# Program order for all engines, with deferred operations, in two attention stages of a two-layer trunk

## Chip, cores and metric

The kernel runs on one core of one Trainium2 chip. The metric is the time of one execution on the device in microseconds (us). "Before" is the median of three runs.

## What is computed

Two layers of a diffusion trunk over 256 context tokens and 256 latent tokens of 1024 channels. In each layer three token mixers read the same normalised input, and gates merge them:

```python
o_a = mla_attend(...)                    # 8 heads
s = einsum(q, k) * dh ** -0.5            # differential attention: 4 heads, two softmaxes each
a = p[:, :, 0] - lam * p[:, :, 1]
o_b = rms_norm(a @ v, diff_norm) * (1 - lam_init)
o_c = swa(...)                           # 8 heads, window 128, context keys and a sink logit
y = (ga * (o_a @ wa) + gb * (o_b @ wb) + gc * (o_c @ wc)) @ wo
x = x + gate * rms_norm(y)
x = x + gate2 * rms_norm(swiglu(...))
```

Latent queries read all 512 keys, context queries the 256 context keys. In the last layer only the latent tokens are queries. The modulation vectors come from a large product of the conditions with `w_ada`.

## The kernel before, in words

All matrices are float32. A weight block (128 x 1024) is loaded into one of three buffers `raw`, cast on ScalarE (ACT) into a high half, and subtracted on VectorE (DVE) for a low half; both go into one of three buffers `hl` (L131, L132). Each product is then three TensorE (PE) products, high by high, high by low, low by high (`mm3`, L262 to L264).

The work is a list of units, each with its weight blocks. `drive` runs units one after another. A unit is a generator that yields its TensorE cost in microseconds (3 x columns / 2400 for each triple); between the yields `drive` lets two other generators advance: a side, here an attention, which gets `ratio` microseconds of its own cost for each microsecond of the unit's, and a filler, which does the modulation products on VectorE (`ada_dve`: L397, L399, with weights `aw`) at a rate of its own (0.42 in layer 0 here).

An attention is a list of steps, one for each head and tile of 128 queries, and two for the two softmaxes or the two heads of a pair. `attend` interleaves their stages: S scores on TensorE into one of two banks `psS`; E the maximum (L669), the exponential (L673) and, at each second step, the normalisation; T transposes into a bank `psT` and a copy back to `pp` (L689 on ScalarE, L691 on VectorE); V the value products (L696, L776) into `psV`; F the last transposes of a head (differential attention). The score cost of a step is keys x 2 / 2400 us, the ratios in the covered stages are R2 = 0.383 and 0.482 (differential, layers 0 and 1) and R3 = 0.541 and 0.896 (sliding). In the differential attention the transposes and values of a tile come three and four steps behind the scores.

Softmax tiles, gates, rotated projections and small temporaries share six rotating buffers `work`. Rotary tiles take two steps on VectorE (L640, L641), two on GpSimd (POOL; L642, L643), and then casts on ScalarE (L972, L134) and subtractions on VectorE (L973, L135) that split them into `dQA`, `sk`, `sQ`. The differential output is normalised with a copy (L837), squares and a power on GpSimd (L839, L288), sums and a multiply on VectorE (L841, L843).

TensorE and SyncE (SP, which issues the loads) run in the order in which the program emits them. For ScalarE, VectorE and GpSimd a planner sorts the instructions at build time by its own estimate of when each is ready, with E and T at a high priority:

```python
ctx.enter_context(tc.manual_schedule(engines={mybir.EngineType.PE, mybir.EngineType.SP}))
...
with tc.high_priority():
    steps[j - 1]["E"]()
```

Of the kernel before, what the change touches and what calls it, by code (L numbers as in the profile page):

```python
# [19 lines left out]
P = 128  # L20
# [67 lines left out]
def trunk(ctx: ExitStack, tc: tile.TileContext, x, cx, b_ada, attn_post,  # L88
# [39 lines left out]
    def split_into(hi, lo, src, scale=None):  # L128

        if scale is None:  # L130
            nc.scalar.copy(hi, src)  # L131
            nc.vector.tensor_tensor(lo, src, hi.bitcast(F32), ALU.subtract)  # L132
        else:
            nc.scalar.activation(hi, src, AF.Copy, scale=scale)  # L134
            nc.vector.scalar_tensor_tensor(lo, src, scale, hi.bitcast(F32), ALU.mult, ALU.subtract)  # L135

    NHL, NRAW = 3, 3
    units, flat, state = [], [], {"load": 0, "split": 0, "next": 0}
# [33 lines left out]
    def do_split(b):  # L172
# [7 lines left out]
        split_into(b["parts"][0], b["parts"][1], raw, b["scale"])  # L180

    def ahead(idx, live, more):

        live += sum(not b["keep"] for b in flat[idx:state["split"]])
        more -= max(0, state["split"] - idx)
        while state["split"] < len(flat):
            b = flat[state["split"]]
            need = state["split"] < idx
            if not need and (more <= 0 or (live >= NHL and not b["keep"])):
                break  # L190
            while state["load"] <= state["split"]:
                do_load(flat[state["load"]])
                state["load"] += 1
            do_split(b)
# [4 lines left out]
        while state["load"] < min(len(flat), state["split"] + NRAW):  # L199
            do_load(flat[state["load"]])  # L200
            state["load"] += 1
# [33 lines left out]

    def drive(n, side=None, ratio=1.0, at=()):

        acc, t, at = 0.0, 0.0, list(at)
        for _ in range(n):
            for cost in run_unit():  # L240
                fillers(cost)
                acc += cost * ratio
                t += cost
                while at and at[0][0] <= t:
                    at.pop(0)[1]()
                while side is not None and acc > 0:
                    v = next(side, None)
                    if v is None:
                        side = None
                    else:  # L250
                        acc -= v
        for _, f in at:
            f()
        if side is not None:
            for _ in side:
                pass
# [319 lines left out]
    def start():  # L576
        def load():
            do_load(flat[state["load"]])
            state["load"] += 1
# [99 lines left out]
    def p_T(st, nk, act, dst=None):  # L679
# [8 lines left out]
        if act:  # L688
            nc.scalar.copy(dst, src)  # L689
        else:  # L690
            nc.vector.tensor_copy(dst, src)  # L691

    def weigh(st, nk, av, v):
        n = nk // P
# [3 lines left out]
    def out_T(o, f, oT, qts, scale=None):  # L698
# [7 lines left out]
        split_into(*[oT[f // 2][:, f % 2, j, 512 - n:512] for j in range(2)], pt[:, :n], scale)  # L706

    L = [{} for _ in range(DEPTH)]
    WARM = 18
    PRM = {"WN": (44, 16), "DU": (5, 7, 8, 15, 13, 16, 21, 22), "ST": (0.46, 1.61), "FR": (0.42, 0.642, 0.21, 0.134),  # L710
# [6 lines left out]
    def head64_steps(l, env, bn, passes, qk, v, sinks, mask):  # L717
# [3 lines left out]
        for f in range(4):  # L721
            hs = {}
            for t in qts:
                nk = 256 if t < 2 else 512
                pair = {}
                for m in range(2):
# [12 lines left out]
                    def E(st=st, h=h, nk=nk, m=m, pair=pair):  # L739
# [7 lines left out]
                        if sinks:  # L747
# [3 lines left out]
                            nc.vector.tensor_tensor(sm, sm, es, ALU.add)  # L751
                        rs = small([P, 2], "rsd")
                        nc.vector.reciprocal(rs, sm)
                        for j in range(2):
                            p = pair[j]["p"][:, :nk]
                            if j:
                                nc.scalar.activation(p, p, AF.Copy, scale=rs[:, j:j + 1])
                            else:
                                nc.vector.tensor_scalar(p, p, rs[:, j:j + 1], None, ALU.mult)  # L759

                    def T(st=st, nk=nk, m=m, t=t, hs=hs):
# [5 lines left out]
                    if m:  # L767
                        def V(f=f, t=t, nk=nk, hs=hs, pair=pair):
                            if t % 2 == 0:
# [8 lines left out]
                            if t == qts[-1]:  # L778
# [3 lines left out]
                                split_into(*[env["oT", bn][f // 2][:, f % 2, j, cs] for j in range(2)], hs["av"][:, cs])  # L782
# [10 lines left out]
    def diff_steps(l, env):  # L793
        qts, nq = env["qts"], len(env["qts"])
        steps = []
        for h in range(4):
            hs = {}
            for i, t in enumerate(qts):
                nk = 256 if t < 2 else 512
                pair = {}  # L800
                for m in range(2):
# [9 lines left out]
                    def E(st=st, nk=nk, m=m, pair=pair):  # L811
# [5 lines left out]
                        rs = small([P, 2], "rsd")  # L817
                        nc.vector.reciprocal(rs, pair["sm"])
                        nc.vector.tensor_tensor(rs[:, 1:2], rs[:, 1:2], env["lam"], ALU.mult)
                        p0, p1 = pair[0]["p"], pair[1]["p"]  # L820
                        nc.vector.tensor_scalar(p1[:, :nk], p1[:, :nk], rs[:, 1:2], None, ALU.mult)
                        nc.vector.scalar_tensor_tensor(p1[:, :nk], p0[:, :nk], rs[:, 0:1], p1[:, :nk], ALU.mult, ALU.subtract)

                    st.update(S=S, E=E)
                    if m == 1:
                        def T(st=st, nk=nk):
                            p_T(st, nk, 1)

                        def V(st=st, h=h, nk=nk, i=i, hs=hs):
# [10 lines left out]
                            ssd = small([P, 4], "ssd")  # L840
                            nc.vector.tensor_reduce(ssd[:, :nq], sq[:, :nq], AX.X, ALU.add)  # L841
                            rq = rsqrt(ssd[:, :nq], nq, P * EPS)
                            nc.vector.tensor_tensor(ob, ob, rq.rearrange("p (t o) -> p t o", o=1).to_broadcast([P, nq, P]), ALU.mult)  # L843
# [8 lines left out]
    def mixers(l):  # L852
# [115 lines left out]
        def stack_k(A, B, r):  # L968

            for m in range(2):  # L970
                rows, other = slice(64 * m, 64 * m + 64), slice(64 - 64 * m, 128 - 64 * m)
                nc.scalar.copy(A[rows, m], r[rows])  # L972
                nc.vector.tensor_tensor(B[rows, m], r[rows], A[rows, m].bitcast(F32), ALU.subtract)  # L973
                (nc.vector, nc.gpsimd)[m].tensor_copy(A[other, m], A[rows, m].bitcast(F32))
# [6 lines left out]
        def stack_q(Q, r, n0):  # L981

            cs = slice(n0, 512)
            for m in range(2):
                rows, other = slice(64 * m, 64 * m + 64), slice(64 - 64 * m, 128 - 64 * m)
                split_into(Q[rows, m, cs], Q[other, m, cs], r[rows, cs], 0.125)
# [15 lines left out]
        def after(h, f, r):  # L1002
# [3 lines left out]
            else:  # L1006
                f(r)
# [86 lines left out]
        def sk(parts):  # L1094
# [4 lines left out]
            stack_k(env["sA"], env["sB"], env["r"])  # L1099
# [14 lines left out]
        def sq(i):  # L1114
            def f(parts):
# [3 lines left out]
                stack_q(env["sQ", i // 2][:, i % 2], env["r"], TQ0)  # L1119
# [53 lines left out]
        def branch_pair(bi, i):  # L1173
            def f(parts):
# [15 lines left out]
                if bi == 2:  # L1190
                    nc.vector.tensor_tensor(g, a, g, ALU.add)
                    split_into(env["mh", i // 4][at], env["ml", i // 4][at], g, 0.5)
            return f

        def branch(bi, i0):
            def f(parts):
# [5 lines left out]
                for j in range(2):  # L1202
# [9 lines left out]
                    if bi == 2:  # L1212
                        nc.vector.tensor_tensor(g, a, g, ALU.add)
                        split_into(env["mh", i // 4][:, i % 4, TQ0:512], env["ml", i // 4][:, i % 4, TQ0:512], g, 0.5)
# [212 lines left out]
    for l in range(DEPTH):  # L1427
# [22 lines left out]
        else:  # L1450
# [3 lines left out]
        drive(count(("gate", "branch", "s")) - 24, attend(diff_steps(l, env), PRM["LD"][1]), PRM["R2"][l])  # L1454
        swa = head64_steps(l, env, "c", 2, lambda h, t, nk: stacked(env["sQ", h % 4 // 2][:, h % 2], env["sA"], env["sB"], h // 4, t, nk),
                           lambda h, k: env["sv"][:, k * P + 64 * (h // 4):k * P + 64 * (h // 4) + 64],
                           True, lambda t: {2: (3, 0), 3: (2, 1)}.get(t))
        drive(PRM["SWA"][l])
        drive(12 - PRM["SWA"][l], attend(swa, PRM["LD"][2]), PRM["R3"][l])
        drive(8)  # L1460
        flush()
# [64 lines left out]
```

## Time and profile before

| | |
|---|---|
| median of three runs | 1481.27 us (1480.56 to 1482.76) |
| profiled execution, its own time | 1483.21 us |
| its span, first to last instruction | 1481.4 us |
| TensorE busy | 1439.1 us (97%) |
| VectorE busy | 971.9 us (66%) |
| ScalarE busy | 684.3 us (46%) |
| GpSimd busy | 175.8 us (12%) |
| granted TensorE clock, mean | 0.995 |

The differential attention of layer 0 starts at about 198 us, its sliding attention at about 344 us, and the stretch that the change covers ends near 495 us. In layer 1 the stretch is about 1068 to 1246 us. Matmul ends are modelled, so an idle time of TensorE is read from the starts of its instructions.

### The profile page before, as it was taken

The numbers are of one execution on the slowest core, as the hardware profiler recorded it, in microseconds if no ns is written. First come the engines' busy times: TensorE is split into PE (matmuls) and PEld (weight loads), VectorE is DVE, ScalarE is ACT, GpSimd is POOL, SyncE is SP. The second block draws the span as 40 slices with busy tenths as digits, with TensorE's granted clock in tenths as the row PEclk, the third lists the DMA queues.
The fourth block names the chain that finished last, engine by engine and source line by source line (L and its number), as shares of the span: only waits on it lengthen the run. The fifth ranks groups of instructions, "written<-read, shape, count | busy, mean of one in ns | idle before, by whom it ended". The sixth has DMA issues, their size and how long they took to land. (4 is left out here: it accounts for less than half of the span.)

```text
span 1481.4 us, 21891 instructions
## 1 busy us (share of the span) xinstructions
PE 1439.1 (97%) x8434; PEld 1215.3 (82%) x8434; DVE 971.9 (66%) x1646; ACT 684.3 (46%) x1265; POOL 175.8 (12%) x245
## 2 busy tenths in 40 slices
PE   8989999999999999999999999999999899999998
PEld 7867878777777889887778888877798899899986
DVE  4676777878785655879773224779577776666654
ACT  5576554444552355223222223665455655544443
POOL 1262001120000010000000000364003100100000
PEclk9999999999999999999999999999999999999999
DMA  9321322233223542666572334333242536566664
GB/s 350 123 79 44 113 86 100 102 112 128 86 85 129 185 142 96 215 216 209 204 229 97 100 100 148 123 111 128 100 136 86 164 100 217 168 227 208 219 208 162
DMA packets 62728, 216.16 MB, mean 146 GB/s; under 512 B 7048, under 2 KB 7584, under 8 KB 62624
## 3 DMA queue, kind: packets, MB, share of 16 engines
q1 hardware_dynamic: 61184, 210.05, 42.3%
q10 hardware_dynamic: 1440, 4.72, 0.8%
q8 instruction: 66, 1.08, 0.3%
q14 instruction: 38, 0.31, 0.1%
HBM read 209.48 MB, written 5.27 MB: 145 GB/s over the span
## 5 line engine op out<-in xcount | busy, mean ns | idle before, releaser
L262 PE MATMUL psg<-hT,hl 128*128 128x512 f32 (+1 forms) x1328 | 470.6, 354 | 0.0
L264 PE MATMUL psg<-hT,hl 128*128 128x512 f32 (+1 forms) x1328 | 449.1, 338 | 1.0 <-DVE hl L132 1.0
L263 PE MATMUL psg<-hT,hl 128*128 128x512 f32 (+1 forms) x1328 | 448.8, 338 | 0.3 <-DVE hT L460 0.3
L132 DVE TENSOR_TENSOR hl<-raw,hl 128x1024 fp32r<-128x1024 f32 (+2 forms) x251 | 311.7, 1242 | 207.7 <-ACT hl L131 206.8
L131 ACT CAST hl<-raw 128x1024 fp32r<-128x1024 f32 (+2 forms) x251 | 259.1, 1033 | 328.7 <-PE psg L264 167.8
L262 PEld LDWEIGHTS psg<-hT,hl 128*128 128x128 f32 x1328 | 252.4, 190 | 38.7 <-issue 15.4
L264 PEld LDWEIGHTS psg<-hT,hl 128*128 128x128 f32 x1328 | 252.3, 190 | 29.4 <-DVE hl L132 1.4
L263 PEld LDWEIGHTS psg<-hT,hl 128*128 128x128 f32 x1328 | 252.9, 190 | 25.6 <-issue 3.6
L399 DVE SCALAR_TENSOR_TENSOR acc<-aw,siluc,acc 128x512 f32<-128x512 f32 x224 | 163.9, 757 | 22.8 <-DMA aw<-in_ada_rest 21.8
L477 POOL TENSOR_SCALAR smy<-ssy 128x1 f32<-128x1 f32 x12 | 4.1, 340 | 709.0 <-ACT work L293 709.0
L673 ACT ACTIVATE work<-psS,nm 128x512 f32<-128x512 f32 (+1 forms) x96 | 59.2, 617 | 59.4 <-DVE nm L669 31.3
L669 DVE TENSOR_REDUCE nm<-psS 128x1 f32<-128x512 f32 (+1 forms) x96 | 57.0, 596 | 22.1 <-PE psS L735 15.6
L684 PE MATMUL psT<-ca,work 128*128 128x128 f32 x400 | 63.5, 273 | 6.7 <-DVE work L759 4.1
L262 PE MATMUL psg<-oT,hl 128*128 128x512 f32 (+1 forms) x192 | 68.5, 357 | 0.0
L264 PE MATMUL psg<-oT,hl 128*128 128x512 f32 (+1 forms) x192 | 65.3, 340 | 1.6 <-DVE hl L132 1.6
L263 PE MATMUL psg<-oT,hl 128*128 128x512 f32 (+1 forms) x192 | 65.1, 339 | 0.0
L684 PEld LDWEIGHTS psT<-ca,work 128*128 128x128 f32 x400 | 48.5, 141 | 17.2 <-issue 7.3
L262 PE MATMUL psg<-hl,hT 128*128 128x256 f32 (+1 forms) x168 | 57.1, 340 | 1.4 <-ACT hT L131 1.4
L673 ACT ACTIVATE work<-psS,nmd 128x512 f32<-128x512 f32 (+1 forms) x48 | 29.6, 618 | 44.8 <-DVE nmd L669 23.6
L264 PE MATMUL psg<-hl,hT 128*128 128x256 f32 (+1 forms) x168 | 48.0, 286 | 0.4 <-DVE hT L132 0.4
L263 PE MATMUL psg<-hl,hT 128*128 128x256 f32 (+1 forms) x168 | 47.7, 284 | 0.0
L689 ACT COPY pp<-psT 128x512 f32<-128x512 f32 (+1 forms) x72 | 36.7, 510 | 19.3 <-PE psT L684 18.8
(319 smaller groups left out, 2514.1 us busy)
## 6 DMA issues: line engine op xcount, KB each, us to landing
raw<-in_blocks SPq DMA_DIRECT2D x262, 512.0 KB, 3.5
aw<-in_ada_rest SPq DMA_DIRECT2D x80, 512.0 KB, 4.5
aw<-in_ada_first SPq DMA_DIRECT2D x16, 512.0 KB, 6.9
xd<-xt ACTq DMA_DIRECT2D x6, 512.0 KB, 2.7
xt<-xd SPq DMA_DIRECT2D x6, 512.0 KB, 4.4
raw<-in_blocks SPq DMA_DIRECT2D x8, 272.0 KB, 5.6
xt<-in_ctx SPq DMA_DIRECT2D x4, 512.0 KB, 3.6
gw<-row SPq DMA_DIRECT2D x4, 512.0 KB, 4.4
```

Source lines behind the costliest of these rows:

```text
L131: nc.scalar.copy(hi, src)
L132: nc.vector.tensor_tensor(lo, src, hi.bitcast(F32), ALU.subtract)
L262: nc.tensor.matmul(ps, lhsT=asl(a[0], k), rhs=bsl(b[0], k), start=st, stop=False)
L263: nc.tensor.matmul(ps, lhsT=asl(a[0], k), rhs=bsl(b[1], k), start=False, stop=False)
L264: nc.tensor.matmul(ps, lhsT=asl(a[1], k), rhs=bsl(b[0], k), start=False, stop=en)
L399: nc.vector.scalar_tensor_tensor(acc[:, s], w[:, k], sc, acc[:, s], ALU.mult, ALU.add)
L477: nc.gpsimd.tensor_scalar(sm, ss[:, 0:1], ss[:, 1:2], D * EPS, ALU.add, ALU.add)
L669: nc.vector.tensor_reduce(nm, ps[:, :nk], AX.X, ALU.max, negate=True)
L673: nc.scalar.activation(st["p"][:, :nk], ps[:, :nk], AF.Exp, bias=nm, accum_out=sm)
L684: nc.tensor.transpose(pt[:, k * P:(k + 1) * P], st["p"][:, k * P:(k + 1) * P], ident)
L689: nc.scalar.copy(dst, src)
```

## The change

From the end of the value projections of the differential attention to eight units into the third branch, in both layers, a `manual_schedule()` without arguments puts every engine in program order. Inside it an operation that needs another engine's result can be emitted later: `defer(dt, f)` puts `f` in a heap, and `passed(cost)`, called with each cost that `drive` sees (unit and side), emits what is due. Whoever needs the result first calls it directly (`pair["rest"]()`, `st["out"]()`), and the end of each `drive` empties the heap. Outside of the two stretches `defer` runs `f` at once.

Deferred by: the normalisation after an exponential 1.0 us (`EL`), the split of a rotated tile 3.5 us (`SL`) and its second operand 0.7 us, low halves of weights loaded ahead 1.3 us, copies of transposed tiles 0.4 us, splits of outputs 0.7 us, the merged output 0.8 us, sums of squares 2.5 us and the multiply after them 2.0 us. The next loads into `raw` are now issued together with the low halves. The ratios and rates are unchanged.

```diff
+    late = {"on": False, "t": 0.0, "n": 0, "todo": []}
+
+    def defer(dt, f):
+        done = []
+        def once():
+            if not done:
+                done.append(1)
+                f()
+        if not late["on"]:
+            once()
+            return once
+        late["n"] += 1
+        heapq.heappush(late["todo"], (late["t"] + dt, late["n"], once))
+        return once
+
+    def passed(cost):
+        late["t"] += cost
+        while late["todo"] and late["todo"][0][0] <= late["t"]:
+            heapq.heappop(late["todo"])[2]()
...
+        hi, lo = b["parts"]
+        nc.scalar.copy(hi, raw)
+        def rest():
+            nc.vector.tensor_tensor(lo, raw, hi.bitcast(F32), ALU.subtract)
+            state["low"] += 1
+            loads()
+        if needed:
+            rest()
+        else:
+            defer(1.3, rest)
+
+    def loads():
+        while state["load"] < min(len(flat), state["low"] + NRAW):
+            do_load(flat[state["load"]])
+            state["load"] += 1
...
             for cost in run_unit():
+                passed(cost)
                 fillers(cost)
...
+        caught_up()
...
+        st["out"] = defer(0.4, lambda: nc.scalar.copy(dst, src) if act else nc.vector.tensor_copy(dst, src))
...
+                        def rest():
+                            rs = small([P, 2], "rsd")
+                            nc.vector.reciprocal(rs, pair["sm"])
...
+                        pair["rest"] = defer(EL, rest)
...
+                            def sums():
+                                ssd = small([P, 4], "ssd")
+                                nc.vector.tensor_reduce(ssd[:, :nq], sq[:, :nq], AX.X, ALU.add)
+                                rq = rsqrt(ssd[:, :nq], nq, P * EPS)
+                                defer(2.0, lambda: nc.vector.tensor_tensor(ob, ob, ...))
+                            defer(2.5, sums)
...
-                f(r)
+                defer(SL, lambda: f(r))
...
-                stack_q(env["sQ", i // 2][:, i % 2], env["r"], TQ0)
+                r = env["r"]
+                defer(SL, lambda: stack_q(env["sQ", i // 2][:, i % 2], r, TQ0))
...
+        late["on"] = True
+        with tc.manual_schedule():
+            drive(count(("gate", "branch", "s")) - 24, attend(diff_steps(l, env), PRM["LD"][1]), PRM["R2"][l])
...
+            drive(8)
+            flush()
+        late["on"] = False
```

## Rows read from the trace of the kernel before

**Rows 1.** The page's part 1: busy time, share of the span, instructions.

```profile
PE 1439.1 (97%) x8434; PEld 1215.3 (82%) x8434; DVE 971.9 (66%) x1646; ACT 684.3 (46%) x1265; POOL 175.8 (12%) x245
```

**Rows 2.** Covered windows: us, busy PE, PEld, DVE, ACT, POOL (count each), clock, DMA, GB/s.

```profile
198.00:495.00 297.00, 286.00 (x1465) 226.20 (x1462) 223.19 (x442) 134.53 (x290) 34.00 (x33) 0.99 0.31 108
1068.00:1246.00 178.00, 170.92 (x1295) 158.17 (x1296) 127.37 (x226) 96.52 (x179) 24.39 (x29) 0.99 0.41 134
```

**Rows 3.** Who waited for whom, TensorE, 198 to 495 us.

```profile
PE psV L696 <- ACT pp L689: 4.0, 3, 3.0
PE psT L684 <- DVE work L759: 3.3, 2, 2.9
```

**Rows 4.** The same view, 1068 to 1246 us.

```profile
PE psg L264 <- DVE hl L132: 2.6, 3, 1.6
PE psS L735 <- ACT work L673: 2.0, 1, 2.0
PE psS L809 <- ACT work L673: 1.9, 1, 1.9
```

**Rows 5.** Busy time by window, a stretch at a lower granted clock.

```profile
291.60:295.20 3.60, 3.17 (x10) 2.71 (x11) 3.60 (x7) 2.10 (x6) 0.00 (x0) 0.53 0.00 0
```

**Rows 6.** Timeline near 288 us: start, duration, instruction, idle before and releaser.

```profile
286.96 0.48 ACT L673 ACTIVATE work<-psS,nmd 128x256 f32<-128x256 f32 x1 [1.74 <-DVE sk L973]
...
289.55 0.69 DVE L843 TENSOR_TENSOR work<-work,rq 128x512 f32<-128x512 f32 x1 [1.17 <-POOL rq L288]
290.15 0.68 DVE L669 TENSOR_REDUCE nmd<-psS 128x1 f32<-128x512 f32 x1
...
290.93 0.69 ACT L673 ACTIVATE work<-psS,nmd 128x512 f32<-128x512 f32 x1 [2.61 <-DVE rsd L819]
...
291.61 0.36 ACT L689 COPY pp<-psT 128x256 f32<-128x256 f32 x1
...
292.03 0.58 PE L696 MATMUL psV<-dv,pp 128*128 128x128 f32 x1 [3.02 <-ACT pp L689]
```

**Rows 7.** Timeline, 346 to 352 us.

```profile
345.93 1.23 DVE L132 TENSOR_TENSOR hl<-raw,hl 128x1024 fp32r<-128x1024 f32 x1
...
348.65 0.88 DVE L397 TENSOR_SCALAR acc<-aw,siluc 128x512 f32<-128x512 f32 x2 [0.52 <-DMA aw<-in_ada_rest]
...
350.44 0.15 DVE L751 TENSOR_TENSOR sm<-sm,es 128x2 f32<-128x2 f32 x1
...
351.99 0.41 PE L684 MATMUL psT<-ca,work 128*128 128x128 f32 x2 [2.90 <-DVE work L759]
```

**Rows 8.** Timeline, 1148 to 1152.5 us.

```profile
1148.20 0.86 ACT L134 ACTIVATE sQ<-work 64x256 fp32r<-64x256 f32 x2 [2.43 <-POOL work L643]
...
1149.08 1.05 ACT L131 CAST hl<-raw 128x1024 fp32r<-128x1024 f32 x1
...
1150.63 1.66 DVE L132 TENSOR_TENSOR hl<-raw,hl 128x1024 fp32r<-128x1024 f32 x1
1151.29 1.59 POOL L643 TENSOR_TENSOR work<-rt,rsh 128x256 f32<-128x256 f32 x1
...
1152.35 0.38 PE L264 MATMUL psg<-oT,hl 128*128 128x256 f32 x1 [1.59 <-DVE hl L132]
```

**Rows 9.** Groups by line and shape, VectorE, 198 to 495 us: busy, mean ns, idle.

```profile
L399 DVE SCALAR_TENSOR_TENSOR acc<-aw,siluc,acc 128x512 f32<-128x512 f32 x70 | 53.0, 768 | 7.0 <-DMA aw<-in_ada_rest 7.0
L132 DVE TENSOR_TENSOR hl<-raw,hl 128x1024 fp32r<-128x1024 f32 x37 | 48.2, 1302 | 15.2 <-ACT hl L131 14.9
...
L669 DVE TENSOR_REDUCE nm<-psS 128x1 f32<-128x256 f32 x16 | 6.6, 419 | 5.6 <-PE psS L735 5.5
...
L671 DVE TENSOR_SCALAR nm<-nm,nsink 128x1 f32<-128x1 f32 x32 | 6.6, 209 | 0.5
```

**Rows 10.** Who waited for whom, ScalarE, 198 to 495 us.

```profile
ACT work L673 <- DVE nmd L669: 20.5, 16, 2.5
ACT work L673 <- DVE nm L671: 14.1, 15, 2.4
```

More of the change, by code (lines that the diff above doesn't have):

```diff
@@ L1 @@
+import heapq
 import math
@@ L191, in ahead @@
             while state["load"] <= state["split"]:
+                if state["load"] >= state["low"] + NRAW:
+                    caught_up()
                 do_load(flat[state["load"]])
                 state["load"] += 1
-            do_split(b)
+            do_split(b, need)
             state["split"] += 1
@@ L198, in ahead @@
                 live += not b["keep"]
-        while state["load"] < min(len(flat), state["split"] + NRAW):
-            do_load(flat[state["load"]])
-            state["load"] += 1
+        loads()
     def run_unit():
@@ L234, in start_fill, with caught_up @@
         fill.update(D=gen, n=rate, acc=0.0)
+    late = {"on": False, "t": 0.0, "n": 0, "todo": []}
[15 more added lines that the diff above has]
+            heapq.heappop(late["todo"])[2]()
+    def caught_up():
+        while late["todo"]:
+            heapq.heappop(late["todo"])[2]()
     def drive(n, side=None, ratio=1.0, at=()):
@@ L254, in drive @@
         if side is not None:
-            for _ in side:
-                pass
+            for v in side:
+                passed(v)
+        caught_up()
     def mm3(ps, a, b, asl, bsl, ks, first=True, last=True):
@@ L577, in load @@
         def load():
-            do_load(flat[state["load"]])
-            state["load"] += 1
+            if state["load"] < state["low"] + NRAW:
+                do_load(flat[state["load"]])
+                state["load"] += 1
         def split():
@@ L687, in p_T @@
             dst = st["pT"] = pairs()[:, :n, 0]
[L688 to L691, printed above, removed]
+        st["out"] = defer(0.4, lambda: nc.scalar.copy(dst, src) if act else nc.vector.tensor_copy(dst, src))
     def weigh(st, nk, av, v):
+        st["out"]()
         n = nk // P
@@ L750, in E, with rest, T @@
                             nc.scalar.activation(es, es, AF.Exp)
[L751 to L761, printed above, removed]
+                        def rest():
+                            if sinks:
+                                nc.vector.tensor_tensor(sm, sm, es, ALU.add)
+                            rs = small([P, 2], "rsd")
+                            nc.vector.reciprocal(rs, sm)
+                            for j in range(2):
+                                p = pair[j]["p"][:, :nk]
+                                if j:
+                                    nc.scalar.activation(p, p, AF.Copy, scale=rs[:, j:j + 1])
+                                else:
+                                    nc.vector.tensor_scalar(p, p, rs[:, j:j + 1], None, ALU.mult)
+                        pair["rest"] = defer(EL, rest)
+                    def T(st=st, nk=nk, m=m, t=t, hs=hs, pair=pair):
+                        pair["rest"]()
                         if t % 2 == 0:
@@ L768, in V @@
                         def V(f=f, t=t, nk=nk, hs=hs, pair=pair):
+                            for j in range(2):
+                                pair[j]["out"]()
                             if t % 2 == 0:
@@ L781, in V @@
                                 cs = slice(qts[0] * P, 512)
-                                split_into(*[env["oT", bn][f // 2][:, f % 2, j, cs] for j in range(2)], hs["av"][:, cs])
+                                split_into(*[env["oT", bn][f // 2][:, f % 2, j, cs] for j in range(2)], hs["av"][:, cs], dt=0.7)
                         st["V"] = V
@@ L985, in stack_q @@
                 rows, other = slice(64 * m, 64 * m + 64), slice(64 - 64 * m, 128 - 64 * m)
-                split_into(Q[rows, m, cs], Q[other, m, cs], r[rows, cs], 0.125)
+                split_into(Q[rows, m, cs], Q[other, m, cs], r[rows, cs], 0.125, 0.7)
         if l:
```

67 lines of the change are left out of this document (36 added, 31 removed).

## Prediction

> **What bounds the kernel now.** I read the page first, then busy time by window, then who waits for whom, then the timeline at the longest waits. The page shows a kernel bound by TensorE: 1439.1 of 1481.4 us busy [rows 1]. So a new order on VectorE, ScalarE and GpSimd can win only what TensorE loses in the two stretches that the change covers, about 198 to 495 us in layer 0 and 1068 to 1246 us in layer 1. The windows give that loss: TensorE is busy 286.00 of 297.00 us and 170.92 of 178.00, so it idles 11.0 and 7.1 us. VectorE is busy 223.19 and 127.37 us, 75% and 72% [rows 2]. The reader is to see a small stake, 18.1 us or 1.2%, and a VectorE with room on average but not everywhere.
>
> The waits name the late work. In layer 0: copies of transposed probabilities, 4.0 us in three waits, and normalised probabilities, 3.3 us in two [rows 3]. In layer 1: low halves of weights 2.6 us, and scores that wait for an exponential 2.0 and 1.9 us [rows 4]. [...] At 0.53 a stretch of 3.6 us loses 0.47 x 3.6 = 1.7 us, three lose 5.1. All idle time and all three dips together are 18.1 + 5.1 = 23.2 us: no reordering in these stretches can win more.
>
> **Why TensorE waits.** Near 288 us the maximum of a score tile (L669) starts at 290.15, right behind a multiply (L843) that stood 1.17 us for GpSimd's power. The exponential (L673) on ScalarE had stood 2.61 us, the copy that TensorE needs (L689) is behind it, and the value product starts 3.02 us late [rows 6]. Near 350 us two first products of the modulation filler (L397), held 0.52 us by a DMA, and more filler stand before the row sums (L751), and a transpose waits 2.90 us [rows 7]. In layer 1 the scaling cast of a rotated query (L134) stands 2.43 us for GpSimd's rope add (L643), with the high half of a weight block (L131) right behind it; the next such turn ends in a low half (L132) for which TensorE stood 1.59 us [rows 8].
>
> **The change, part by part.** No arithmetic is added or removed, and TensorE's own order stays, since its instructions were already in program order; only the three other engines' order and the loads' place on SyncE move.
>
> 1. *Sums of squares 2.5 us and the multiply 2.0 us behind.* GpSimd's power gets its time before VectorE reaches the multiply. Taking the multiply from before the maximum saves its wait and slot, 290.15 - 289.55 + 1.17 = 1.8 us; at most the whole 3.0 goes [rows 6]. What is late next is the burst of key splits ahead of it, which the change also shifts. I take 2.4, the middle, and half of the dip behind it, 0.85.
> 2. *Normalisation 1.0 us behind its exponential, filler at its own rate.* In program order the filler yields 1.52 us of products for each 1.52/0.42 = 3.6 us of main work, so one pair can stand before the sums where two pairs stood. One pair less is 0.77 x 2 = 1.5 us [rows 9]; at most 2.9 goes [rows 7]. I take 2.2 and half of that dip, 0.85.
> 3. *Rotated tiles split 3.5 us behind.* Rope needs two VectorE steps, then GpSimd's two; the visible add runs 1.59 us. The weight's high half now goes ahead of the casts, which were 2.43 us of wait and 0.86 of work in front of it [rows 8]. That is more than the 1.59 us lost, so all low-half waits go: 2.6 us [rows 4]. Bounds 1.6 and 2.6.
> 4. *Low halves 1.3 us behind the casts, loads behind the low halves.* A load into a raw buffer had to wait for the low half that read it anyway; so its place behind it on SyncE costs nothing, and a modulation load that was queued behind it may go earlier. The cover is three raw buffers; without it a block's DMA would add to each unit. 0, with the 0.5 us of the DMA wait in [rows 7] as bound either way.
> 5. *Copies 0.4, splits of outputs 0.7, merged outputs 0.8 us behind.* They sit behind their transposes as before. I take 0; bounds: the remaining 1.0 us of [rows 3] gained, and 0.4 us lost at each of the differential attention's 24 value products (4 heads x 4 tiles, then 4 x 2), 9.6 us, if the copy were always the last to arrive. It is not: it was late three times.
> 6. *The remaining waits* (18.1 - 3.0 - 2.9 - 2.6 = 9.6 us) are dealt anew. I take them as they were; bounds 0 and, with the third dip, 9.6 + 1.7 gained.
> 7. *What the fixed order costs.* Before, the maximum of a score tile could overtake a low half (1.30 us) or filler products (0.77 each); now it stands behind any that the program put earlier [rows 9]. ScalarE already stands 20.5 + 14.1 us in layer 0 for these maxima [rows 10], of which TensorE feels little: its longest such waits are the 2.0 + 1.9 us of layer 1 [rows 4]. I take 2.5 more, two thirds of these 3.9. Bounds: 0, and 25.6 (next part).
>
> Sum: gains 2.4 + 0.85 + 2.2 + 0.85 + 2.6 = 8.9, cost 2.5, net -6.4 us. The profiled execution took 1483.2 us (its span and 1.8 around it), 1.9 above the median of the runs; so 1476.8 for it, and 1481.27 - 6.4 = 1474.9, taken as **1475**, for a median.
>
> [...] A low half lasts 1.23 us at 345.93 us and 1.66 at 1150.63, where a GpSimd add of 1.59 us runs beside it [rows 7, 8]: 0.43 us more. [...] By the rows it has some 2.4 + 0.86 us more room than before, so I keep -6.4.
>
> **The rivals.**
>
> *VectorE in a fixed order becomes the bound (slower).* Place: the short tiles (256 keys) of layer 0. By the program's costs the scores of such a step take 256 x 2/2400 = 0.21 us, with 0.21/0.383 = 0.56 us of main work after them (0.383 is its ratio in layer 0), and a transpose group as much again: 2 x (0.21 + 0.56) = 1.5 us from one score tile to the next. The maximum (0.42, [rows 9]) and its exponential (0.48, [rows 6]) with hand-overs need 1.0. So 0.5 us is spare, and a low half of 1.30 us in front loses 0.8. There are 4 heads x 2 tiles x 2 = 16 such diff steps and 16 sliding ones, which also have an extra step of 0.21 (L671) [rows 9]. All 32 lose 25.6 us, half of them 12.8. For it: VectorE is already 75% busy over the whole stretch [rows 2]. Against: a maximum may start as soon as its own scores are done, a step before that point, which gives 1.5 us more. It decides from 11 lost steps (8.9/0.8). Time: 1481.3 - 8.9 + 12.8 to 25.6 = 1485 to 1498.
>
> *The waits only move (no change).* The work tiles rotate through six buffers, and the deferred splits hold a rotated tile 3.5 us longer. An exponential already stood 1.74 us for the split that frees its tile [rows 6]. At the ten rope units, with TensorE feeling half of it, that is 8.7 us, which cancels the 8.9. Against it: the steps that free most work tiles, transposes on TensorE, are not deferred. A low half stretched by 0.43 us in each of these units works the same way. Time: 1479 to 1484.
>
> *Everything goes (much faster).* If program order with these distances suits the chip as a whole, step 6 is won too: 18.1 + 5.1 = 23.2 at most, two thirds of it 15.5: 1458 to 1466. For it: most of the long waits stand behind work that was needed later. Against: nine of the eighteen microseconds have no single cause that the change names.
>
> **How the numbers follow.** Forecast: 0.44. Much faster: 0.12. No change: 0.15. Slower: 0.29. The likeliest is 1475. Its own range: steps 1 to 3 at their lower ends give 1.8 + 1.5 + 1.6 = 4.9, less 2.5 a gain of 2.4; at their upper ends with both dips, 3.0 + 1.7 + 2.9 + 1.7 + 2.6 = 11.9, and nothing lost: 1469 to 1479. The whole range, 1461 to 1491, takes in half of the slower rival's span and more than half of the much faster one's, and leaves out some 0.05 below and 0.13 above. About 0.2%, 3.0 us, is what a measurement of this kernel can tell from no change: faster 0.56, same 0.15, slower 0.29.
>
> **What would show it.** Step 1: no wait of TensorE above 1.5 us for L689's copy, and VectorE's multiply (L843) no longer idle before GpSimd's power. Step 2: no transpose waiting over 1.5 us for L759. Step 3: no waits for L132 in layer 1's rope units, and L131 before L134 in ScalarE's order. Dips: one or none in the two stretches. Step 7: the waits of score products for L673; should they exceed today's by 8.9 us, the fixed order has taken back what it gave. The prediction is wrong if VectorE's idle time falls while TensorE's grows (VectorE the bound), if exponentials wait for splits or copies that free their tiles (buffers), or if the listed waits vanish and the time stays (the loss was in hand-overs that no wait shows).

## The result and the profile after

The kernel with the change takes 1500.35 us (median of four runs, 1499.51 to 1502.03) beside 1481.37 (1480.56 to 1482.76) of the kernel before: a ratio of 1.0131, 95% interval 1.0118 to 1.0145. It is 19.0 us slower, where 6.4 us faster was forecast, and lies above the range too. The profiled execution took 1499.51 us, its span 1497.7.

The page of the kernel after, busy time by engine, beside [rows 1]:

```profile
PE 1443.6 (96%) x8434; PEld 1213.2 (81%) x8434; DVE 978.1 (65%) x1646; ACT 686.1 (46%) x1265; POOL 176.3 (12%) x245
```

The counts are the same; TensorE's busy time grew by 4.5 us of the span's 16.3. The rest is idle time. Busy time by window, after: the two stretches that the change covers (first two lines, beside [rows 2]; the first is longer, and the second runs later by what was lost ahead of it), then three stretches of low granted clock (beside [rows 5]). Columns as in [rows 2].

```profile
198.00:512.00 314.00, 290.96 (x1457) 226.27 (x1456) 232.41 (x447) 133.82 (x289) 35.33 (x33) 0.98 0.31 105
1080.00:1262.00 182.00, 173.70 (x1319) 159.46 (x1318) 131.48 (x229) 100.23 (x182) 23.29 (x29) 1.00 0.39 130
203.10:206.50 3.40, 3.35 (x8) 2.67 (x9) 2.63 (x9) 0.56 (x2) 0.00 (x0) 0.51 0.71 252
322.60:329.50 6.90, 5.21 (x15) 4.29 (x16) 3.93 (x8) 2.03 (x4) 1.40 (x2) 0.51 0.33 120
411.30:414.80 3.50, 3.50 (x17) 1.65 (x16) 1.11 (x2) 0.00 (x0) 0.00 (x0) 0.51 0.02 5
```

TensorE idles 314.00 - 290.96 = 23.0 us in layer 0 (before 11.0) and 8.3 in layer 1 (before 7.1, in a window 4 us shorter). The granted clock is 0.51 in these three. In the second, products of 128x512 start every 0.43 us (325.60 to 329.02), right behind it every 0.23. TensorE is busy 12.06 us of the three stretches, 13.8 us long, and loses, as an estimate from the clock, 0.49 x 12.06 = 5.9 us. Before there were the stretch of [rows 5] and two more:

```profile
353.20:356.70 3.50, 3.50 (x12) 2.77 (x10) 3.43 (x7) 1.30 (x4) 0.00 (x0) 0.52 0.02 5
1097.20:1100.80 3.60, 3.60 (x16) 3.41 (x17) 2.75 (x7) 2.01 (x5) 0.73 (x2) 0.53 0.07 9
```

The two of layer 0 lost 0.47 x 3.17 + 0.48 x 3.50 = 3.2 us, estimated the same way; layer 1 has none now. TensorE runs the same instructions in the same order in both kernels, so the time between the same two of them can be compared: in layer 0 the stretch grew from 304.6 to 322.4 us, in layer 1 from 180.2 to 180.9. **All but 0.7 us of the loss is in layer 0**: 12.0 of its 17.8 us are idle time, 2.7 the clock. The other 3 are put down to the waits too, as an estimate from one of them. TensorE stands 25 times in this stretch (over 0.03 us each), 12 times before. Its products of 128x512 overlap (start to start 0.23 us, lasting 0.39). Around the wait for L747 at 306.2 us, in the kernel after, they don't: the next start comes 0.60 us later, before 0.23, but only 0.20 of it counts as idle time, since ends are modelled; 0.11 more is lost right behind.

Who waited for whom, TensorE, layer 0 after (198 to 512 us; us in total, times, longest), beside [rows 3]. The change moved lines: L669 is now L728 (maximum), L671 L730 (clamp), L673 L732 (exponential), L735 and L809 are L793 and L875 (scores), L689 is L747 (copy), L759 L820 (normalised), L843 L916 (the multiply).

```profile
PE psS L793 <- ACT work L732: 7.7, 8, 1.5
PE psS L875 <- ACT work L732: 5.5, 6, 1.6
PE psT L759 <- DVE work L916: 4.7, 1, 4.7
PE psT L743 <- DVE work L820: 4.3, 5, 1.6
PE psV L753 <- ACT pp L747: 0.5, 2, 0.3
```

The same view of layer 1 after (1080 to 1262 us), beside [rows 4]:

```profile
PE psS L793 <- ACT work L732: 4.6, 3, 2.1
PE psT L743 <- DVE work L820: 1.2, 2, 0.9
PE psS L875 <- ACT work L732: 1.0, 2, 0.6
```

The waits that the change aimed at are gone or small: copies 4.0 to 0.5 us, low halves in layer 1 2.6 to none. Two others took their place: scores that wait until an exponential has read the bank that they are to fill, 13.2 us in layer 0 (1.3 before), and one transpose that waits 4.7 us for the multiply behind the power.

Behind the score waits stands VectorE. Who waited for whom, ScalarE, layer 0 after, beside [rows 10]: 87 us where 34.6 were.

```profile
ACT work L732 <- DVE nmd L728: 49.7, 30, 4.0
ACT work L732 <- DVE nm L730: 37.3, 22, 4.1
```

And groups by line and shape, VectorE, layer 0 after, beside [rows 9]:

```profile
L457 DVE SCALAR_TENSOR_TENSOR acc<-aw,siluc,acc 128x512 f32<-128x512 f32 x74 | 56.3, 802 | 0.0
L193 DVE TENSOR_TENSOR hl<-raw,hl 128x1024 fp32r<-128x1024 f32 x39 | 48.3, 1239 | 30.1 <-ACT hl L190 30.0
...
L728 DVE TENSOR_REDUCE nmd<-psS 128x1 f32<-128x256 f32 x16 | 6.7, 416 | 0.0
L728 DVE TENSOR_REDUCE nm<-psS 128x1 f32<-128x256 f32 x16 | 6.6, 415 | 0.4 <-PE psS L793 0.4
```

The last number is idle time ahead of the instruction. Before, VectorE stood 5.6 us in front of one group of short maxima, waiting for scores [rows 9]; now it stands 0.4 us for the same group. It no longer waits for scores, because it comes to nearly every maximum after they are done. Instead it stands 30.1 us in front of low halves, nearly all of it for ScalarE's casts (15.2 before). From the two traces, the start of each maximum minus the (modelled) end of the last product of its scores, as a mean over the stretch: before 0.82 us in layer 0 and 0.40 in layer 1, after **3.49** and 3.21. Of the 64 x 3.49 = 223 us that layer 0's maxima are late, filler products hold 51 us and low halves 37. One such place in the timeline after (start, duration, instruction, idle before and releaser):

```profile
251.76 0.28 PE L875 MATMUL psS<-dB,dQA 128*128 128x256 f32 x1
...
252.45 1.23 DVE L193 TENSOR_TENSOR hl<-raw,hl 128x1024 fp32r<-128x1024 f32 x1 [0.70 <-ACT hl L190]
253.60 1.41 DVE L457 SCALAR_TENSOR_TENSOR acc<-aw,siluc,acc 128x512 f32<-128x512 f32 x2
...
254.92 0.42 DVE L728 TENSOR_REDUCE nmd<-psS 128x1 f32<-128x256 f32 x1
255.43 0.47 ACT L732 ACTIVATE work<-psS,nmd 128x256 f32<-128x256 f32 x1 [3.01 <-DVE nmd L728]
...
256.05 0.38 PE L875 MATMUL psS<-dQA 128*128 128x256 f32 x1 [1.49 <-ACT work L732]
```

The scores are done at 252.0. Ahead of their maximum in VectorE's order are a low half, which itself waits 0.70 us for a cast, and two filler products: it starts at 254.92, the exponential stood 3.01 us, and the scores that need the bank come 1.49 us late.

The other new wait, in the timeline after, at the end of the fourth head of the differential attention:

```profile
318.93 0.67 DVE L914 TENSOR_REDUCE ssd<-work 128x4 f32<-128x512 f32 x1
...
319.59 1.72 POOL L702 TENSOR_TENSOR work<-rt,rsh 128x256 f32<-128x256 f32 x1
...
321.39 0.55 POOL L344 TENSOR_SCALAR rs<-ssd 128x4 f32<-128x4 f32 x1
322.03 1.39 POOL L346 TENSOR_TENSOR rq<-rs,mhalf 128x4 f32<-128x4 f32 x1
...
323.45 0.69 DVE L916 TENSOR_TENSOR work<-work,rq 128x512 f32<-128x512 f32 x1 [0.93 <-POOL rq L346]
...
324.29 1.09 PE L759 MATMUL psT<-ca,work 128*128 128x128 f32 x4 [4.71 <-DVE work L916]
```

The sums (L914) come just behind a rope, whose add on GpSimd (L702) now stands ahead of the power (L344, L346). TensorE waits 4.71 us, and the low clock begins in that wait (1.00 from 322.0 to 322.4 us, 0.77 in the next 0.4 us, with no product before 324.29).

### The profile page after: what moved, and what is told of

Read it like the earlier page. It is cut to its first block, busy times and chain, and to the rows that moved or that the text cites. A ratio compares the mean times of both kernels' runs of the same rounds, so it can differ in the third digit from the quotient of the medians.

```text
span 1497.7 us, 21878 instructions
## 1 busy us (share of the span) xinstructions
PE 1443.6 (96%) x8434; PEld 1213.2 (81%) x8434; DVE 978.1 (65%) x1646; ACT 686.1 (46%) x1265; POOL 176.3 (12%) x245
## 5 line engine op out<-in xcount | busy, mean ns | idle before, releaser
L193 DVE TENSOR_TENSOR hl<-raw,hl 128x1024 fp32r<-128x1024 f32 (+2 forms) x251 | 307.6, 1226 | 224.9 <-ACT hl L190 224.0
L322 PEld LDWEIGHTS psg<-hT,hl 128*128 128x128 f32 x1328 | 252.4, 190 | 27.9
L732 ACT ACTIVATE work<-psS,nm 128x512 f32<-128x512 f32 (+1 forms) x96 | 59.2, 617 | 83.9 <-DVE nm L730 50.1
L728 DVE TENSOR_REDUCE nm<-psS 128x1 f32<-128x512 f32 (+1 forms) x96 | 57.0, 595 | 18.2 <-PE psS L793 17.9
L732 ACT ACTIVATE work<-psS,nmd 128x512 f32<-128x512 f32 (+1 forms) x48 | 29.6, 618 | 67.3 <-DVE nmd L728 64.8
L747 ACT COPY pp<-psT 128x512 f32<-128x512 f32 (+1 forms) x72 | 36.6, 509 | 23.7 <-PE psT L743 23.3
```

Source lines behind the costliest of these rows:

```text
L193: nc.vector.tensor_tensor(lo, raw, hi.bitcast(F32), ALU.subtract)
L322: nc.tensor.matmul(ps, lhsT=asl(a[1], k), rhs=bsl(b[0], k), start=False, stop=en)
L728: nc.vector.tensor_reduce(nm, ps[:, :nk], AX.X, ALU.max, negate=True)
L732: nc.scalar.activation(st["p"][:, :nk], ps[:, :nk], AF.Exp, bias=nm, accum_out=sm)
L747: st["out"] = defer(0.4, lambda: nc.scalar.copy(dst, src) if act else nc.vector.tensor_copy(dst, src))
```

## The experiments

Two theories stood at first. *Late maxima*: the program emits maximum and exponential (E) of a step one step behind its scores; the planner lifted them, a fixed order keeps them there, on VectorE. *Distances*: the deferrals themselves put something too late. Medians are beside runs of the kernel before on the same chip (1481.64 to 1483.06); "delay" is the delay of a maximum behind its scores, worked out as above, layer 0 / layer 1.

**Order without distances, distances without order, VectorE left to the planner, E early.** Four edits of the kernel after (engine names are shortened, and early_max is shown for the two stretches only):

```diff
 order_only
-        late["on"] = True
 dist_only
-        with tc.manual_schedule():
+        with ExitStack():
 dve_free
-        with tc.manual_schedule():
+        with tc.manual_schedule(engines={PE, SP, Activation, Pool}):
 early_max
-                steps[j]["S"]()
-            if 0 <= j - 1 < n:
-                with tc.high_priority():
-                    steps[j - 1]["E"]()
...
+                    steps[j - 1]["soon"]()
+                if j < n:
+                    steps[j]["S"]()
+                    steps[j]["soon"] = defer(EM, steps[j]["E"])
...
-    EL, SL = 1.0, 3.5
+    EL, SL, EM = 1.0, 3.5, 0.3
```

> Program order on all engines in both stretches, but nothing deferred. Theory A (in a fixed order the maximum of a score tile stands behind all that the program put between its scores and it; in the trace of the changed kernel it starts some 3.4 us after its scores, 0.4 to 1.2 before): the deferral is not the cause, so at least as slow as the changed kernel, 1498 to 1515 us, with score waits of TensorE of 20 us or more. Rival B (the deferred operations hold buffers and banks too long): about 1482.

Measured: 1556.47 us, ratio 1.0501 (1.0483 to 1.0520); delay 4.24 / 4.81. TensorE's waits, order_only, 195 to 515 us:

```profile
PE psS L875 <- ACT work L732: 18.1, 9, 3.8
PE psS L793 <- ACT work L732: 13.4, 12, 2.3
```

> The distances alone, with the planner still ordering ScalarE, VectorE and GpSimd in both stretches. Theory A: the planner lifts the maximum, so 1476 to 1486 us and score waits of 4 to 8 us. Rival B (deferral holds buffers and banks): 1495 to 1502, as the changed kernel.

Measured: 1481.63 us, 0.9996 (0.9986 to 1.0007); delay 0.58 / 0.53.

> As the changed kernel, but VectorE is ordered by the planner; ScalarE, GpSimd, TensorE and SyncE in program order. Theory A: most of the loss goes, 1478 to 1488 us. Rival C (ScalarE's or GpSimd's fixed order is the cause): stays at 1494 to 1502.

Measured: 1475.75 us, 0.9953 (0.9935 to 0.9971); delay 0.61 / 0.34.

> As the changed kernel, but the stage with the maximum and the exponential is emitted 0.3 us of work after its own scores, in place of one whole step later. Theory A: score waits of TensorE fall from 20 us to under 8, 1482 to 1490 us; the 4.7 us wait of the last transposes of the fourth differential head stays. Rival B (buffers): no better, as the exponential's tiles are held longer, 1498 or more.

Measured: 1502.44 us, 1.0128 (1.0108 to 1.0149); delay 1.27 / 1.38. TensorE's waits, early_max, 195 to 515 us:

```profile
PE psV L760 <- ACT pp L754: 7.6, 7, 2.3
PE psT L766 <- DVE work L923: 3.5, 1, 3.5
PE psV L849 <- ACT pp L754: 3.3, 3, 1.3
PE psT L750 <- DVE mod L382: 1.4, 1, 1.4
PE psS L882 <- ACT work L739: 1.1, 2, 0.8
PE psT L750 <- DVE work L827: 0.7, 2, 0.5
PE psS L800 <- ACT work L739: 0.6, 1, 0.6
```

What follows: the distances are not the loss. Without them the fixed order costs 75 us, they give 56 of these back, and under the planner they change nothing in sum. The order of VectorE alone is worth 1500.35 - 1475.75 = 24.6 us: with it given back to the planner, the other two engines in program order and the distances are 6.0 us *better* than before. But early_max missed: its score waits are down to 1.7 us in layer 0, and its time did not move. Between the same instructions its layer 0 is 7.9 us shorter than that of the kernel after, and its layer 1 6.5 us longer. ScalarE runs in order too, and an exponential emitted early stands, waiting for its maximum, in front of the copies (L754) that TensorE needs for the value products: they are now waited for 10.9 us in layer 0 and 9.9 in layer 1. So E holds two operations that want different places.

**What lies ahead of a maximum, and the end of the fourth head.** fill_behind emits filler only right behind an E, late_f makes the empty steps behind the last scores of the differential attention 0.6 us long where they are 0.2, and thin_after and thin_before leave seven of eight filler products out for three modulation vectors of layer 0, in the kernel after and before:

```diff
 late_f
-            yield (steps[j]["cost"][0] if j < n else 0.2) + ...
+            yield (steps[j]["cost"][0] if j < n else 0.6 if late["on"] and d == 9 else 0.2) + ...
 fill_behind
-                fillers(cost)
+                late["credit"] += cost
+                if not late["on"] or side is None or late["go"]:
+                    fillers(late["credit"])
+                    late.update(credit=0.0, go=False)
...
                     steps[j - 1]["E"]()
+                late["go"] = True
 thin_after, thin_before
-                        else:
+                        elif l or kind not in (0, 2, 3, 4):
```

> As the changed kernel, but the empty tail steps of the differential attention last 0.6 us of side cost in place of 0.2, so that the fourth head's last transposes come 5 x 0.4/0.383 = 5 us later. Theory D (one distance is too short: that head's transposes wait 4.7 us for the multiply, which stands behind GpSimd's power and rope, and 6.8 us at half clock follow): 4.7 + 3.4 = some 8 us less than the changed kernel, 1491 to 1494. Theory A (VectorE's backlog in its fixed order): the backlog shows again elsewhere, and under 4 us are won, 1496 to 1500.

Measured: 1493.23 us, 1.0076 (1.0056 to 1.0096). The wait for the multiply is gone.

> As the changed kernel, but inside the stretches the modulation filler is emitted only right behind a maximum and its exponential, never between the scores and their maximum. Theory A: filler products are the largest part of what stands before the maxima in layer 0 (51 us over 64 maxima), so they start about 1 us sooner and half of layer 0's loss goes: 1486 to 1493 us. Rival E (only the low halves and ScalarE's casts matter): 1497 to 1502.

Measured: 1489.08 us, 1.0049 (1.0033 to 1.0065); delay 3.20 / 3.13.

> The changed kernel with seven of eight products of the modulation filler left out for three vectors of layer 0 (the output is then not the reference's); the loads stay. Theory A: VectorE has room again in layer 0, whose part of the loss (about 15 us) mostly goes, layer 1's stays: 1480 to 1488 us. Rival E (the fixed order alone is to blame, whatever VectorE's load): within 4 us of the changed kernel.

Measured: 1480.60 us, 0.9992 (0.9983 to 1.0002); delay 2.46 / 3.21.

> The kernel before with the same products left out, as the yardstick for the run above. TensorE bounds it and the planner puts the products into gaps, so little is won: 1472 to 1480 us. The difference of the two thinned kernels is the price of the fixed order without that load: under 9 us by theory A, 15 to 20 by its rival.

Measured: 1471.29 us, 0.9932 (0.9917 to 0.9946); delay 0.38 / 0.45.

What follows: late_f confirms the second wait as a cause of its own, worth 7.1 us. With less filler the change costs 1480.60 - 1471.29 = 9.3 us where it costs 19.0 with all of it: VectorE's load of filler so sets about half of the price; these runs do not part filler ahead of the maxima from other filler. fill_behind gained 11.3 us, but the maxima start only 0.3 us sooner on average. Filler right behind the E of the last step still stands between the scores of this step and their maximum; so its mechanism, as stated, is not shown. Its trace shows where the gain lies: the maxima that start over 5 us late fall from 13 to 7 of layer 0's 64, score waits from 13.2 to 6.8 us, the wait for the multiply from 4.7 to 2.0.

**Combinations, and VectorE alone in order.** free_late_f is dve_free with late_f, fill_late_f is fill_behind with late_f, low_behind puts the low halves that are not yet needed behind an E as well, and dve_fixed fixes VectorE alone and leaves ScalarE and GpSimd to the planner:

```diff
 low_behind (on fill_late_f)
-            defer(1.3, rest)
+            late["lows"].append((late["t"], defer(2.5, rest)))
...
+                for x in [x for x in late["lows"] if late["t"] - x[0] >= 1.0]:
+                    late["lows"].remove(x)
+                    x[1]()
 dve_fixed
-        with tc.manual_schedule():
+        with tc.manual_schedule(engines={PE, SP, DVE}):
```

> VectorE ordered by the planner as in dve_free, and the tail of the differential attention stretched as in late_f. In dve_free the fourth head's last transposes still wait 3.1 us for their multiply, and 3.4 us at half clock follow. Theory D: 3.1 + 1.7 = some 4.8 us less than dve_free, 1469 to 1473 us, the fastest so far. Theory A alone (the order of VectorE was all): 1474 to 1477.

Measured: 1477.26 us, 0.9965 (0.9953 to 0.9977); a score wait of 4.4 us is new.

> All engines in program order with both fill_behind's filler place and late_f's tail. If the two causes are separate, the gains add: 7 + 11 of the loss of 19, 1480 to 1484 us. If fill_behind had won mostly the same tail event (its wait there fell from 4.7 to 2.0 us), only some 3 more: 1485 to 1488.

Measured: 1495.50 us, 1.0096 (1.0079 to 1.0114); one wait of 5.5 us for a low half is new, in layer 1.

> As fill_late_f, and the low halves that are not needed yet also right behind a maximum and its exponential (at least 1.0 and at most 2.5 us of work after their casts). They are the second largest part of what stands before the maxima (37 us over 64). If what counts is how much stands before a maximum, another 3 to 6 us: 1476 to 1480. If it is the casts on ScalarE that VectorE waits for (11 us of its idle time there), later low halves win about the same; if neither, within 2 us of fill_late_f.

Measured: 1488.89 us, 1.0048 (1.0032 to 1.0064); delay 2.99 / 2.94, and a low half is still waited for 5.6 us.

> The mirror of dve_free: VectorE in program order with all distances, ScalarE and GpSimd ordered by the planner. Theory A: VectorE's order is the cause, so as slow as the changed kernel or slower, 1497 to 1510 us. Rival C (two engines that are both fixed block each other in turns, and one free engine is enough): 1478 to 1488.

Measured: 1504.96 us, 1.0156 (1.0135 to 1.0177); delay 3.51 / 2.74.

What follows: dve_fixed settles which engine it is. VectorE in order is as slow by itself as all three, so what ScalarE and GpSimd do is not the cause. The others missed what was expected, and show that small gains don't add: late_f was worth 7.1 us alone and nothing on dve_free, and fill_behind lost some 6 with it. Each shift deals one or two single waits of 3 to 6 us anew. That is why the delays, means over 64 maxima in layer 0, are read beside the times; a mean hides its longest cases, though, as fill_behind shows.

**The maximum alone.** If the exponential must stay and the maximum must come, they are to be parted. M is the maximum with its clamp, emitted 0.3 us behind S; E keeps the exponential and its place, and emits M first if it is still due:

```diff
 split_max
                 steps[j]["S"]()
+                if late["on"]:
+                    steps[j]["max"] = defer(EM, steps[j]["M"])
...
+    def softmax_max(ps, nk, nm, floor=None):
+        nc.vector.tensor_reduce(nm, ps[:, :nk], AX.X, ALU.max, negate=True)
+        if floor is not None:
+            nc.vector.tensor_scalar(nm, nm, floor, None, ALU.min)
...
+                    def M(st=st, nk=nk):
+                        st["nm"] = small([P, 1], "nmd", bufs=4)
+                        softmax_max(st["ps"], nk, st["nm"])
...
+                        if "max" in st:
+                            st["max"]()
 split_only (on split_max): no other distance
-        if not late["on"]:
+        if not late["on"] or dt != EM:
```

split_late_f is split_max with late_f; split_dve_fixed and early_dve_fixed are split_max and early_max with VectorE alone in order.

> All engines in program order with all distances; the maximum alone (and its clamp by the sink) is emitted 0.3 us of work after its scores, while the exponential stays one step behind. Theory A (the maximum's place in VectorE's order): maxima start about 1.3 us after their scores in place of 3.4, the copies on ScalarE keep their place, score waits under 8 us: 1482 to 1490 us. Theory F (VectorE is late with everything in a fixed order, and the waits only move to the next consumer, here normalised probabilities and copies): 1495 to 1503.

Measured: 1478.62 us, 0.9977 (0.9961 to 0.9994); delay 0.77 / 0.52. Its TensorE waits from 195 to 505 us, and VectorE's groups from 198 to 505:

```profile
PE psT L752 <- DVE work L836: 6.1, 7, 2.0
PE psT L768 <- DVE work L940: 4.2, 1, 4.2
PE psS L891 <- ACT work L741: 1.1, 2, 0.8
PE psT L752 <- DVE pp L756: 0.9, 1, 0.9
PE psS L802 <- ACT work L741: 0.6, 1, 0.6
```

```profile
L730 DVE TENSOR_REDUCE nm<-psS 128x1 f32<-128x512 f32 x16 | 11.0, 687 | 5.3 <-PE psS L804 5.2
L730 DVE TENSOR_REDUCE nmd<-psS 128x1 f32<-128x512 f32 x16 | 11.0, 685 | 1.3 <-PE psS L891 1.1
L730 DVE TENSOR_REDUCE nm<-psS 128x1 f32<-128x256 f32 x16 | 6.7, 416 | 2.8 <-PE psS L802 2.8
L730 DVE TENSOR_REDUCE nmd<-psS 128x1 f32<-128x256 f32 x16 | 6.6, 417 | 3.3 <-PE psS L891 3.3
```

> As split_max, with ScalarE and GpSimd ordered by the planner (as in dve_fixed, 1505 us). Theory A: 1482 to 1492. Theory F: 1497 to 1508.

Measured: 1481.45 us, 1.0001 (0.9990 to 1.0011); delay 0.81 / 0.45.

> As early_max (maximum and exponential 0.3 us after the scores), with ScalarE and GpSimd ordered by the planner. If early_max lost its gain only because ScalarE's fixed order put copies behind exponentials, 1480 to 1490 us; by theory F 1495 to 1505.

Measured: 1477.09 us, 0.9971 (0.9959 to 0.9982); delay 1.25 / 1.54.

> All engines in program order, the maximum 0.3 us of work behind its scores, and every other operation emitted at once, without distance. The distances were worth 56 us with the maximum one step behind (1556 against 1500). If they matter as much by themselves, 1515 to 1535; if most of that was the maximum standing behind stalled operations, 1485 to 1505.

Measured: 1497.72 us, 1.0103 (1.0084 to 1.0121); delay 1.95 / 2.14.

> split_max with the stretched tail of the differential attention. Its last transposes wait 4.2 us in split_max. If that event is a cost of its own, it goes: 1470 to 1475 us, the fastest so far. If the moved products re-deal other waits, 1475 to 1482.

Measured: 1471.36 us, 0.9921 (0.9907 to 0.9935); delay 0.77 / 0.52. Its busy time by window:

```profile
195.00:495.00 300.00, 291.28 (x1500) 230.30 (x1501) 233.23 (x450) 136.80 (x295) 36.16 (x33) 0.99 0.34 114
1065.00:1250.00 185.00, 182.65 (x1373) 168.61 (x1370) 141.34 (x239) 104.32 (x186) 22.50 (x29) 1.00 0.46 149
```

What follows: one small operation (two with the clamp) moved in the text, and nothing else, wins 1500.35 - 1478.62 = 21.7 us. VectorE waits for scores again (12.4 us in the four groups), the score waits of TensorE fall from 13.2 to 1.7 us, and VectorE alone in order, 1504.96, becomes 1481.45. early_dve_fixed says the same from the other side: the early E that won nothing with ScalarE in order wins 27.9 us on dve_fixed when the planner may sort ScalarE. And split_only says that the distances are needed too: 19.1 us of split_max are theirs. With the end of the fourth head mended, split_late_f beats both kernels, by 11.7 us the one before. In its windows TensorE idles 8.7 and 2.4 us, and one stretch of low clock is left (0.50 from 422 to 424 us) of three before.

The layers differ. Between the same instructions layer 0 took 304.6 us before, 322.4 after, 305.5 in split_max and 299.4 in split_late_f; layer 1 (1068 to 1246 us before) 178.0, 178.6, 172.7 and 172.0. So late maxima cost some 6 us in layer 1 as well, which the change's own gains there hid in its net 0.7.

## Why the prediction was wrong

The step that failed is **step 7, what the fixed order costs**: 2.5 us taken, 24.6 measured as VectorE's order alone (dve_free against the kernel after). It knew that a maximum was free to overtake before and that "now it stands behind any that the program put earlier", and it named the signal: score waits that exceed the old ones by 8.9 us. They went from 1.3 to 13.2 us in layer 0 and from 3.9 to 5.6 in layer 1, 13.6 more. What it did not do was read, in the steps of `attend`, how much the program puts earlier. E of step j - 1 comes behind S of step j, so ahead of each maximum stands a whole step's share of filler, low halves and normalisations. Instead it took two thirds of the longest waits seen under the planner (3.9 us). Rows of the planner's order could not price an order that the planner had hidden; the upper bound of 25.6 came near the measured 24.6 by luck, since it was worked out from layer 0's short steps alone, and layer 1, which has none, shows maxima 3.21 us late too.

The slower rival named the right engine and the right sign, with a chance of 0.29. Its time, 1485 to 1498, was still 2.4 us short. Its place was too narrow: it counted only steps of 256 keys that lack spare time. Nor did VectorE become the bound: the sign set for that, less idle time on it, did not come (297.00 - 223.19 = 73.8 us before [rows 2], 314.00 - 232.41 = 81.6 after). Its order cost the time, not its load alone. And the argument that held it back, "a maximum may start as soon as its own scores are done, a step before that point", is what the program's order forbids: layer 0's maxima started on average 3.49 us behind their scores.

*Step 1* was half right. Waits for the copy L747 fell to 0.5 us as named. But the deferral of 2.5 and 2.0 us counts costs that pass, and at the end of the fourth head the steps passed are empty and 0.2 us each; the multiply moved behind a rope and its power, and a wait of 4.7 us and 6.9 us of low clock took the place of 3.0 and one dip (a stretch of low clock). late_f prices it at 7.1 us, more than the 2.4 + 0.85 that the step promised. VectorE was to stand no more for the power; it stands 0.93 us at the place shown.

*Step 2*: the two waits with a longest of 2.9 us became five with a longest of 1.6, in total 4.3 where they were 3.3. The long one went, the sum did not.

*Step 3* did what it said: no low half of a weight is waited for in layer 1. Idle time between the same instructions still grew, from 7.0 to 7.6 us: score waits grew by 1.7 and transposes that wait for L820 by 1.0. The low halves did not get slower, as the rival of moved waits had it with its 0.43 us: 39 took 1239 ns on average in layer 0, where 37 took 1302 before [rows 9]. Beside GpSimd some do take longer: before, the 8 that ran beside a GpSimd instruction for over 0.3 us took 1602 ns, the other 29 1220. But after, only 4 ran so, for 1380 ns: the deferral made the meetings rarer, not more frequent.

*Steps 4 and 5* at zero are borne out by their own rows: the filler's 7.0 us of waits for DMA [rows 9] are 0.0, and TensorE waits 0.5 us for copies. *Dips*: "one or none" was wrong, three in layer 0, and none in layer 1. The 1.7 us of a dip, with the 0.85 taken twice and the 5.1 of three, is an estimate from the clock and the length of [rows 5]; no run measures a dip by itself. By the same estimate the dips of layer 0 took 5.9 us after, 3.2 before. *The other rivals* had nothing: no wait of TensorE above is for a work buffer, on ScalarE exponentials wait 3.7 us for a transpose that frees one (5.6 before), and "everything goes" needed the maxima in time.

Not settled: why a later place for the filler shortens the longest delays in fill_behind and leaves the middle one at 3.2 us.

## What to carry to other kernels

Before a planner's order is replaced by the program's, take from the trace how far each short, urgent operation stands behind its input, and see where the program's text puts the same operation: what a priority had lifted (here a maximum that lasts 0.4 to 0.7 us, and whose place was worth 22 us) must be moved in the text. Part such an operation from the one that consumes it on the next engine, since an early consumer can block its own queue, as the exponential blocked the copies (10.9 us of TensorE's waits in layer 0 of early_max). And a distance counted in emitted work is only as long as the steps it passes; look at the ends of loops, where they are empty.

## What the hardware showed that was not expected

That VectorE, 74% busy in layer 0's stretch (232.41 of 314.00 us), can cost TensorE 25 us over both layers by order alone, while in split_late_f it is 78% busy (233.23 of 300.00) and TensorE idles 8.7. In the program's order the maxima of layer 0 start 3.49 us on average behind finished scores, with other work in front; before it was 0.82.

Low clock appeared in the stretch of layer 0 in four traces (before two stretches, after three, split_max two, split_late_f one). All but one of these last some 3.5 us at a granted clock near 0.5. Before, the stretches of 291.6, 353.2 and 1097.2 us begin in or up to 1.2 us behind waits of 3.02, 2.90 and 1.88 us; the one of 6.9 us in the kernel after began while TensorE stood 4.71 us. TensorE was busy 5.21 us of it, so that wait cost, by the estimate from the clock, 0.49 x 5.21 = 2.6 us more than its own length. Not every long wait is followed by one: behind 2.09 us at 1178.9 us after there is none (1.00 from 1178 to 1190 us).
